# Filter units of a Hyena layer: whole fp32 transforms, small weights loaded on both partition halves, second buffers

## The chip, the cores and the metric

The kernel runs on one core of a Trainium2 chip. The metric is the device time of one execution in microseconds; lower is better. A core has TensorE (PE in the profile; its weight loads are PEld), VectorE (DVE), ScalarE (ACT) and GpSimd (POOL) for the work, and SyncE (SP), whose queue issues most of the transfers. Each engine works through its own instructions in order, and waits on semaphores where it needs another's result.

## What is computed

A trunk of two layers over 512 latent tokens and 256 context tokens, D = 1024, all in float32. Layer 0 is attention (a latent kind and a grouped-query kind side by side), layer 1 a Hyena mixer; each is followed by an MLP with squared ReLU and hidden width 4096. The change touches the part that prepares the Hyena filters:

```python
def hyena_filters(L, f_w1, f_b1, f_w2, f_b2, f_w3, f_b3, f_freq, f_w4):
    ...                                   # feats -> three sine layers -> h: (L, 64)
    h = (h @ f_w4.astype(F32)).reshape(L, 2, HYENA_ORDER, D_MODEL)
    ...
    h = h * window[:, None, None, :]
    h = h * lax.rsqrt(jnp.sum(h * h, axis=(0, 1), keepdims=True) + EPS)
    return h[:, 0], h[:, 1]

def bidir_long_conv(u, hf, hb, skip):
    L = u.shape[1]
    kfull = jnp.concatenate([hf, jnp.zeros_like(hf[:1]), hb[:0:-1]], axis=0)
    K = jnp.fft.rfft(kfull, n=2 * L, axis=0)
    U = jnp.fft.rfft(uf, n=2 * L, axis=1)
    y = jnp.fft.irfft(U * K[None], n=2 * L, axis=1)[:, :L]
    return (y + uf * skip.astype(F32)).astype(u.dtype)
```

There are two such convolutions, one after the other (orders n = 0 and 1), over all 1024 columns. `K` depends on the weights alone, not on the tokens.

## The kernel before

**Products.** Most products of the kernel are made of three products in a reduced format, fp32r: an operand is split into a part `hi` that fp32r holds and the remainder `lo`, and `mm3` (L107) adds hi x hi, hi x lo and lo x hi. A weight block is split by `split_w`: ScalarE casts `whi` (L125), VectorE subtracts to get `wlo` (L126). Activations are split by `split_to`: a cast (L169) and a subtraction (L172), which gives tiles such as `mHhi` and `mHlo` of the MLP's hidden values.

**Filter units.** The spectra `K` are made in eight units, one for each order n and each block c of 256 columns (`filter_unit`, from L984). A unit runs in steps:

1. It loads a row of `h_skip`, two blocks of `h_f_w4` (into `w4raw`, 64 partitions) and a block of the window. For the sum of the two directions (i = 0) it adds them to `w4s`, splits that into `w4hi` and `w4lo` on 64 partitions, and ScalarE copies both halves to partitions 64 to 127 (L1003, L1004), since the other operand `h3st` holds its high part in the lower and its remainder in the upper partitions. Eight products follow (L1012, L1013), and VectorE multiplies with the window into `eo0` (L1014).
2. The same for the difference (i = 1), into `eo1`. The tiles `w4s`, `w4hi`, `w4lo`, `w4raw`, `eo0` and `eo1` have one buffer each.
3. Squares and their sums (L1021, L1023); `eo0` and `eo1` are split into `eohi` and `eolo`.
4. The norm: one product (L1033), then a reciprocal root, and `skip` and `fy` are scaled.
5. The transforms to even and odd frequencies: twelve `mm3`, 36 products, of `eohi`/`eolo` with the tables `Tfhi`/`Tflo`, and one product of the `skip` row (L1060). VectorE makes the even part `kE` (L1065).
6. ScalarE copies the odd part `kO`, GpSimd merges both into `Kout` by four additions (L929), multiplies all with `fy` (L1072), and issues the store to DRAM (L1073). The Hyena layer reads it later.

**What sets the order.** The units lie beside the MLP of layer 0. The MLP gives out its products in blocks of 24, and after each block calls `tick` (L80), which takes one step from the list of background work. That is `zip_bg` (L1354): with each tick one step of the modulation for layer 1 (`mod_chunks`: a load of 512 KB, `modw`, on SyncE's queue, and one multiply-add on VectorE, L368 or L370) and one step of the filter units. So between the steps of a unit TensorE has one or two blocks of 24 MLP products. A scheduler then sets the order of instructions on each engine from the program's order and its own estimates. The transform tables are loaded by GpSimd's queue when the units begin.

Of the kernel before, what the change touches and what calls it, by code (L numbers as in the profile page):

```python
# [9 lines left out]
F32 = mybir.dt.float32  # L10
F32R = mybir.dt.float32r
AF = mybir.ActivationFunctionType
ALU = mybir.AluOpType
AX = mybir.AxisListType
P = 128

D, S, C, FF = 1024, 512, 256, 4096
# [48 lines left out]
def f(ap):  # L66
    return ap.bitcast(F32)


class Kernel:  # L70
# [839 lines left out]

    def load_tables(self, pool, inverse):

        nc, src = self.nc, self.a["k_dft"]
        res = []
        if inverse:
            for nm, sl in (("Tf", slice(0, 8)), ("Ti", slice(10, 22))):
                t = pool.tile([P, sl.stop - sl.start, P], F32, name=nm, bufs=1)
                nc.sync.dma_start(out=t, in_=src[:, 2, sl])
                res.append(t)
            return res  # L920
        t = Split(pool.tile([P, 10, P], F32R, name="Tfhi", bufs=1), pool.tile([P, 10, P], F32R, name="Tflo", bufs=1))
        nc.gpsimd.dma_start(out=t.hi, in_=src[:, 0, 0:10])
        nc.gpsimd.dma_start(out=t.lo, in_=src[:, 1, 0:10])
        return [t]

    def merge(self, U, E, O, e0, e1):

# [56 lines left out]
    def filter_unit(self, fp, T, n, c, kdst):  # L984

        nc, a = self.nc, self.a
        ch = slice(256 * c, 256 * c + 256)
        wf = fp.tile([65, 2, 256], F32, name="w4raw", bufs=1)
        nc.sync.dma_start(out=wf[64:65, 0], in_=a["h_skip"][0, n:n + 1, ch])
        for dr in range(2):  # L990
            nc.sync.dma_start(out=wf[0:64, dr], in_=a["h_f_w4"][0][:, (dr * 2 + n) * D + 256 * c:(dr * 2 + n) * D + 256 * c + 256])
        win = fp.tile([P, 4, 256], F32, name="win", bufs=1)
        nc.sync.dma_start(out=win, in_=a["k_win"][:, :, ch])
        skip = fp.tile([1, 256], F32, name="skip", bufs=2)
        nc.scalar.copy(skip, wf[64:65, 0])
        eo, spl = [], []
        for i, op in enumerate((ALU.add, ALU.subtract)):
            ws = fp.tile([64, 256], F32, name="w4s")
            nc.vector.tensor_tensor(out=ws, in0=wf[0:64, 0], in1=wf[0:64, 1], op=op)
            w2 = Split(fp.tile([P, 256], F32R, name="w4hi"), fp.tile([P, 256], F32R, name="w4lo"))  # L1000
            nc.scalar.copy(w2.hi[0:64], ws)
            nc.vector.tensor_tensor(out=w2.lo[0:64], in0=ws, in1=f(w2.hi[0:64]), op=ALU.subtract)
            nc.scalar.copy(w2.hi[64:128], f(w2.hi[0:64]))  # L1003
            nc.scalar.copy(w2.lo[64:128], f(w2.lo[0:64]))  # L1004
            e = fp.tile([P, 4, 256], F32, name=f"eo{i}", bufs=1)
            for t2 in range(2):
                ps = self.sm()
                for tt in range(2):
                    r = 2 * t2 + tt
                    lhs = self.h3[:, r * P:(r + 1) * P]  # L1010
                    o = ps[:, 256 * tt:256 * tt + 256]
                    nc.tensor.matmul(o, lhs, w2.hi, start=True, stop=False)  # L1012
                    nc.tensor.matmul(o, lhs, w2.lo, start=False, stop=True)  # L1013
                nc.vector.tensor_tensor(out=e[:, 2 * t2:2 * t2 + 2], in0=ps.rearrange("p (t n) -> p t n", t=2),  # L1014
                                        in1=win[:, 2 * t2:2 * t2 + 2], op=ALU.mult)
            eo.append(e)
            yield
# [6 lines left out]

        nc.vector.tensor_tensor(out=eo[0][0:1, 0], in0=eo[0][0:1, 0], in1=eo[1][0:1, 0], op=ALU.add)
        nc.vector.tensor_scalar(out=eo[0][0:1, 0], in0=eo[0][0:1, 0], scalar1=0.5, scalar2=None, op0=ALU.mult)
        for i in range(2):
            s = Split(fp.tile([P, 4, 256], F32R, name="eohi", bufs=2), fp.tile([P, 4, 256], F32R, name="eolo", bufs=2))
            self.split_to(s, eo[i])
            spl.append(s)  # L1030
        yield
        pn = self.sm()
        nc.tensor.matmul(pn, self.ones, sq[0], start=True, stop=True)  # L1033
# [16 lines left out]
        for b in (1, 0):  # L1050
            for i in (1, 0):
                o = pe[b][:, 256 * i:256 * i + 256]
                self.mm3(o, T[:, 4 * b + i], spl[i][:, 2 * b], True, bool(b or i))
        po = [self.sm() for _ in range(2)]
        for b in range(2):
            for i in range(2):
                q, cs = po[b][:, 256 * i:256 * i + 256], (i + b) % 2
                self.mm3(q, T[:, 2 + cs], spl[i][:, 1], True, False)
                self.mm3(q, T[:, 6 + 2 * b + cs], spl[i][:, 3], False, True)
        nc.tensor.matmul(o, self.ones[0:1], skip, start=False, stop=True)  # L1060
        c = fp.tile([P, 512], F32, name="kO1", bufs=1)
        nc.scalar.copy(c, pe[1])
# [340 lines left out]

def _r12(x):

    u = np.ascontiguousarray(x, np.float32).view(np.uint32).astype(np.uint64)
    u = (u + 0x7FF + ((u >> 12) & 1)) >> 12 << 12
    return u.astype(np.uint32).view(np.float32)  # L1410


def _tables():
    t = {}
    cst = np.zeros((P, 544), np.float32)
# [16 lines left out]
    for i, w in enumerate((HD, RP)):  # L1432
        nf = w // 4
        inv = (np.float32(10000.0) ** (-np.arange(nf, dtype=np.float32) / np.float32(nf))).astype(np.float32)
        for p in range(P):
            e = p % w
# [11 lines left out]
    tabs = [fn(ang(r)).T for r in range(4) for fn in (np.cos, np.sin)]  # L1448
    tabs += [-tabs[6], -tabs[7]]
    for eo in range(2):  # L1450
        for fn in (np.cos, np.sin):
            tabs += [fn(ang(eo)), fn(ang(eo + 2)), -fn(ang(eo + 2))]
    m = np.stack(tabs, 1).astype(np.float64)
    hi = _r12(m.astype(np.float32))
    t["k_dft"] = np.ascontiguousarray(np.stack([hi, _r12((m - hi).astype(np.float32)), m.astype(np.float32)], 1))

    tt = np.arange(S, dtype=np.float32)
    tn = tt / np.float32(S)
# [35 lines left out]
```

## Time and profile before

| | us |
|---|---|
| Median of 3 runs | 1568.7 (1565.3 to 1571.17) |
| Profiled execution | 1564.55 |
| Span of the trace | 1562.8 |
| TensorE busy in the span | 1449.0 (93%) |
| VectorE busy | 1109.5 (71%) |
| ScalarE busy | 699.7 (45%) |
| GpSimd busy | 403.1 (26%) |

The mean granted clock of TensorE is 0.976 of its full 2.4 GHz. The eight filter units lie between about 452 and 812 us of the span. In the profile an instruction is shown with its line, the tile that it writes, the tiles that it reads, and behind it in brackets the time that its engine stood idle before it and what ended that. `128*128 128x512` on a product is weights by moving columns; a product in plain fp32 is shown as two records.

### The profile page before, as it was taken

The page shows a single profiled execution, that of the slowest core. Times are in us where ns is not written, and L with a number is a line of the kernel's source. Part 1 is how long each engine was busy: PE and PEld are TensorE (multiplying, and loading weights), DVE is VectorE, ACT ScalarE, POOL GpSimd, SP SyncE. Part 2 cuts the span into 40 slices and gives each one's busy share as a digit, 9 for nine tenths or more (in the row PEclk, how much of TensorE's full clock was granted, in tenths as well). Part 3 has the DMA queues.
Part 4 walks back from the last instruction along what each step waited for, and adds up shares of the span by engine and source line. Part 5 has one row for each costly group of instructions (what it writes and reads, how often), then busy time and mean ns, then how long its engine had stood idle before and what let it go on. Part 6 is the DMA issues. An engine that isn't in the chain of part 4 may idle for free. (4 is left out here: it accounts for less than half of the span.)

```text
span 1562.8 us, 19761 instructions
## 1 busy us (share of the span) xinstructions
PE 1449.0 (93%) x7468; PEld 1192.0 (76%) x7468; DVE 1109.5 (71%) x1582; ACT 699.7 (45%) x1140; POOL 403.1 (26%) x340
## 2 busy tenths in 40 slices
PE   8688899999989999989999979999987999999998
PEld 2356588888877777878789967788776888888898
DVE  3898899887688988898765659798847434344454
ACT  3534587766653344344425444434325413232242
POOL 0440235232320322232220345445354000000001
PEclk9899999999999999999999989999998999999999
DMA  8557200221346655564334323231222223233241
GB/s 314 196 176 224 48 1 21 59 53 50 109 157 232 202 191 175 175 198 159 121 108 162 110 86 106 84 108 41 95 91 72 81 81 108 87 102 104 85 135 55
DMA packets 134461, 186.06 MB, mean 119 GB/s; under 512 B 16584, under 2 KB 117709, under 8 KB 131294
## 3 DMA queue, kind: packets, MB, share of 16 engines
q1 hardware_dynamic: 132192, 174.62, 34.6%
q0 software_dynamic: 1440, 9.70, 1.8%
q8 instruction: 59, 0.97, 0.3%
q10 hardware_dynamic: 734, 0.48, 0.1%
q14 instruction: 36, 0.29, 0.1%
HBM read 171.67 MB, written 10.49 MB: 117 GB/s over the span
## 5 line engine op out<-in xcount | busy, mean ns | idle before, releaser
L125 ACT CAST whi<-wraw 128x1024 fp32r<-128x1024 f32 (+3 forms) x211 | 198.9, 949 | 360.4 <-PE sm L110 341.1
L126 DVE TENSOR_TENSOR wlo<-wraw,whi 128x1024 fp32r<-128x1024 f32 (+2 forms) x195 | 241.4, 1242 | 105.8 <-ACT whi L125 95.8
L110 PE MATMUL sm<-h_lo,whi 128*128 128x512 f32 (+1 forms) x720 | 275.6, 384 | 3.9 <-POOL h_lo L424 3.1
L109 PE MATMUL sm<-h_hi,whi 128*128 128x512 f32 (+1 forms) x720 | 276.4, 387 | 2.2 <-ACT h_hi L420 2.2
L111 PE MATMUL sm<-h_hi,wlo 128*128 128x512 f32 (+1 forms) x720 | 274.1, 382 | 3.6 <-DVE wlo L126 3.6
L110 PE MATMUL sm<-mHlo,whi 128*128 128x512 f32 (+1 forms) x640 | 223.5, 349 | 6.0 <-DVE mHlo L172 6.0
L109 PE MATMUL sm<-mHhi,whi 128*128 128x512 f32 (+1 forms) x640 | 225.9, 353 | 0.5 <-ACT whi L125 0.3
L111 PE MATMUL sm<-mHhi,wlo 128*128 128x512 f32 (+1 forms) x640 | 223.2, 349 | 1.9 <-DVE wlo L126 1.9
L835 DVE SCALAR_TENSOR_TENSOR xT<-sm,mod,xT 128x512 f32<-128x512 f32 (+1 forms) x136 | 83.7, 621 | 150.7 <-PE sm L111 150.5
L110 PEld LDWEIGHTS sm<-h_lo,whi 128*128 128x128 f32 x720 | 136.0, 189 | 32.9 <-POOL h_lo L424 5.5
L111 PEld LDWEIGHTS sm<-h_hi,wlo 128*128 128x128 f32 x720 | 135.8, 189 | 32.1 <-DVE wlo L126 6.1
L109 PEld LDWEIGHTS sm<-h_hi,whi 128*128 128x128 f32 x720 | 134.8, 189 | 30.7 <-ACT h_hi L420 2.8
L110 PEld LDWEIGHTS sm<-mHlo,whi 128*128 128x128 f32 x640 | 121.7, 190 | 22.5 <-DVE mHlo L172 7.0
L111 PEld LDWEIGHTS sm<-mHhi,wlo 128*128 128x128 f32 x640 | 121.5, 190 | 18.7 <-DVE wlo L126 3.4
L109 PEld LDWEIGHTS sm<-mHhi,whi 128*128 128x128 f32 x640 | 121.4, 190 | 18.2 <-issue 1.7
L929 POOL TENSOR_TENSOR Kout<-kE,kO 128x512 f32<-128x512 f32 x32 | 46.3, 1471 | 264.6 <-DVE kE L1065 264.6
L370 DVE SCALAR_TENSOR_TENSOR modacc<-modw,silu,modacc 128x1024 f32<-128x1024 f32 x63 | 84.1, 1335 | 27.4 <-DMA modw<-in_w_mod 27.2
L1126 POOL TENSOR_TENSOR zx<-zx,zt 128x384 f32<-128x384 f32 x64 | 79.4, 1260 | 93.1 <-ACT zt L1124 91.8
L639 POOL TENSOR_SCALAR prob<-prob,smx 128x768 f32<-128x768 f32 x64 | 60.4, 943 | 146.9 <-DVE smx L638 91.8
L1245 POOL TENSOR_TENSOR facc<-facc,fsq 128x256 f32<-128x256 f32 x12 | 9.5, 790 | 333.1 <-ACT fsq L1243 333.1
L169 ACT CAST mHhi<-ms 128x512 fp32r<-128x512 f32 x64 | 39.6, 620 | 79.8 <-DVE ms L875 79.5
L637 ACT ACTIVATE prob<-big,smx,qry 128x768 f32<-128x768 f32 x64 | 63.7, 997 | 11.8 <-DVE smx L635 11.2
(458 smaller groups left out, 3002.4 us busy)
## 6 DMA issues: line engine op xcount, KB each, us to landing
wraw<-in_mlp_w SPq DMA_DIRECT2D x67, 1024.0 KB
modw<-in_w_mod SPq DMA_DIRECT2D x80, 512.0 KB
wraw<-in_h_w_in SPq DMA_DIRECT2D x12, 1024.0 KB
wm<-in_w_mod SPq DMA_DIRECT2D x8, 1024.0 KB
kd<-Kout POOLq DMA_DIRECT2D x8, 1024.0 KB, 5.4
Kin<-kd SPq DMA_DIRECT2D x8, 1024.0 KB
wraw<-in_a_w_in SPq DMA_DIRECT2D x5, 1024.0 KB
wraw<-in_a_w_out SPq DMA_DIRECT2D x9, 512.0 KB
```

The lines of the kernel that those rows point to most:

```text
L109: mm(ps, w.hi, x.hi, start=first, stop=False)
L110: mm(ps, w.hi, x.lo, start=False, stop=False)
L111: mm(ps, w.lo, x.hi, start=False, stop=last)
L125: nc.scalar.copy(hi, r3)
L126: (lo_eng or nc.vector).tensor_tensor(out=lo, in0=r3, in1=f(hi), op=ALU.subtract)
L169: nc.scalar.copy(dst.hi, src)
L370: nc.vector.scalar_tensor_tensor(out=acc, in0=w, scalar=s, in1=acc, op0=ALU.mult, op1=ALU.add)
L637: nc.scalar.activation(out=p, in_=sf, func=AF.Exp, bias=sm[:, 1:2], scale=sc, accum_out=sm[:, 2:3])
L639: nc.gpsimd.tensor_scalar(out=p, in0=p, scalar1=sm[:, 3:4], scalar2=1.0, op0=ALU.mult, op1=ALU.mult)
L835: nc.vector.scalar_tensor_tensor(out=xt, in0=ps, scalar=gcol[:, d:d + 1], in1=xt, op0=ALU.mult, op1=ALU.add)
L929: tt = lambda e, o, x, y, op: e.tensor_tensor(out=o, in0=x, in1=y, op=op)
L1126: nc.gpsimd.tensor_tensor(out=t[:, o0:o0 + n], in0=t[:, o0:o0 + n], in1=b[:, i0:i0 + n], op=ALU.add)
```

## The change

It does four things in the filter units:

- The transforms of step 5 are twelve products in plain fp32 rather than twelve `mm3`. The splits of `eo0` and `eo1` in step 3 are gone. The table is loaded once, in fp32 (`Tf`), by SyncE's queue, instead of `Tfhi` and `Tflo` by GpSimd's.
- `w4raw` has 128 partitions. Four loads bring each block of `h_f_w4` to both halves of the partitions; the sum or difference, the cast and the subtraction run over 128 partitions, and ScalarE's copies from half to half are gone. The row of `h_skip` comes by a load of its own rather than by way of `w4raw` and a copy.
- `w4raw`, `w4hi` and `w4lo` have two buffers.
- `eo0` and `eo1` have two buffers.

The rest of the diff follows from that: the table of the Hyena layer's own transforms is read from the same, smaller array.

```diff
     def load_tables(self, pool, inverse):
 
-        nc, src = self.nc, self.a["k_dft"]
         res = []
-        if inverse:
-            for nm, sl in (("Tf", slice(0, 8)), ("Ti", slice(10, 22))):
-                t = pool.tile([P, sl.stop - sl.start, P], F32, name=nm, bufs=1)
-                nc.sync.dma_start(out=t, in_=src[:, 2, sl])
-                res.append(t)
-            return res
-        t = Split(pool.tile([P, 10, P], F32R, name="Tfhi", bufs=1), pool.tile([P, 10, P], F32R, name="Tflo", bufs=1))
-        nc.gpsimd.dma_start(out=t.hi, in_=src[:, 0, 0:10])
-        nc.gpsimd.dma_start(out=t.lo, in_=src[:, 1, 0:10])
-        return [t]
+        for nm, sl in (("Tf", slice(0, 8)), ("Ti", slice(10, 22))) if inverse else (("Tf", slice(0, 10)),):
+            t = pool.tile([P, sl.stop - sl.start, P], F32, name=nm, bufs=1)
+            self.nc.sync.dma_start(out=t, in_=self.a["k_dft"][:, sl])
+            res.append(t)
+        return res
...
-        wf = fp.tile([65, 2, 256], F32, name="w4raw", bufs=1)
-        nc.sync.dma_start(out=wf[64:65, 0], in_=a["h_skip"][0, n:n + 1, ch])
+
+        wf = fp.tile([P, 2, 256], F32, name="w4raw", bufs=2)
         for dr in range(2):
-            nc.sync.dma_start(out=wf[0:64, dr], in_=a["h_f_w4"][0][:, (dr * 2 + n) * D + 256 * c:(dr * 2 + n) * D + 256 * c + 256])
+            for h in range(2):
+                nc.sync.dma_start(out=wf[64 * h:64 * h + 64, dr],
+                                  in_=a["h_f_w4"][0][:, (dr * 2 + n) * D + 256 * c:(dr * 2 + n) * D + 256 * c + 256])
         win = fp.tile([P, 4, 256], F32, name="win", bufs=1)
         nc.sync.dma_start(out=win, in_=a["k_win"][:, :, ch])
         skip = fp.tile([1, 256], F32, name="skip", bufs=2)
-        nc.scalar.copy(skip, wf[64:65, 0])
-        eo, spl = [], []
+        nc.sync.dma_start(out=skip, in_=a["h_skip"][0, n:n + 1, ch])
+        eo = []
         for i, op in enumerate((ALU.add, ALU.subtract)):
-            ws = fp.tile([64, 256], F32, name="w4s")
-            nc.vector.tensor_tensor(out=ws, in0=wf[0:64, 0], in1=wf[0:64, 1], op=op)
-            w2 = Split(fp.tile([P, 256], F32R, name="w4hi"), fp.tile([P, 256], F32R, name="w4lo"))
-            nc.scalar.copy(w2.hi[0:64], ws)
-            nc.vector.tensor_tensor(out=w2.lo[0:64], in0=ws, in1=f(w2.hi[0:64]), op=ALU.subtract)
-            nc.scalar.copy(w2.hi[64:128], f(w2.hi[0:64]))
-            nc.scalar.copy(w2.lo[64:128], f(w2.lo[0:64]))
-            e = fp.tile([P, 4, 256], F32, name=f"eo{i}", bufs=1)
+            ws = fp.tile([P, 256], F32, name="w4s")
+            nc.vector.tensor_tensor(out=ws, in0=wf[:, 0], in1=wf[:, 1], op=op)
+            w2 = Split(fp.tile([P, 256], F32R, name="w4hi", bufs=2), fp.tile([P, 256], F32R, name="w4lo", bufs=2))
+            self.split_to(w2, ws)
+            e = fp.tile([P, 4, 256], F32, name=f"eo{i}", bufs=2)
...
-        for i in range(2):
-            s = Split(fp.tile([P, 4, 256], F32R, name="eohi", bufs=2), fp.tile([P, 4, 256], F32R, name="eolo", bufs=2))
-            self.split_to(s, eo[i])
-            spl.append(s)
...
-                self.mm3(o, T[:, 4 * b + i], spl[i][:, 2 * b], True, bool(b or i))
+                nc.tensor.matmul(o, T[:, 4 * b + i], eo[i][:, 2 * b], start=True, stop=bool(b or i))
...
-                self.mm3(q, T[:, 2 + cs], spl[i][:, 1], True, False)
-                self.mm3(q, T[:, 6 + 2 * b + cs], spl[i][:, 3], False, True)
+                nc.tensor.matmul(q, T[:, 2 + cs], eo[i][:, 1], start=True, stop=False)
+                nc.tensor.matmul(q, T[:, 6 + 2 * b + cs], eo[i][:, 3], start=False, stop=True)
```

In the changed code the lines from L916 on are lower: `kE` is made at L1054, GpSimd's product with `fy` is L1061, the product of `skip` L1049, and the products with `w4lo` L1006.

On TensorE, the end of the first unit's transforms before; the numbers behind the tiles tell buffers apart:

```order
L109 MATMUL sm_5101<-eohi_4995,Tfhi_4816 128x256
L110 MATMUL sm_5101<-eolo_4996,Tfhi_4816 128x256
L111 MATMUL sm_5101<-eohi_4995,Tflo_4817 128x256
L109 MATMUL sm_5101<-eohi_4999,Tfhi_4816 128x256
L110 MATMUL sm_5101<-eolo_5000,Tfhi_4816 128x256
L111 MATMUL sm_5101<-eohi_4999,Tflo_4817 128x256
L1060 MATMUL sm_5086<-skip_4870,ones_79 128x256
```

The same place after:

```order
L1047 MATMUL sm_5080<-eo0_4877,Tf_4816 128x256
L1048 MATMUL sm_5080<-eo0_4877,Tf_4816 128x256
L1047 MATMUL sm_5080<-eo1_4925,Tf_4816 128x256
L1048 MATMUL sm_5080<-eo1_4925,Tf_4816 128x256
L1049 MATMUL sm_5073<-skip_4869,ones_79 128x256
```

Three products have become one, which reads `eo` itself; the blocks of the MLP around them stand as before.

On VectorE, around the first unit's `kE` before. `xT` is the stream that the MLP adds to, `modacc` the modulation's sum, and `w4lo_5244` the remainder for the second unit's second group of products:

```order
L368 TENSOR_SCALAR modacc_6083<-modw_6084,silu_105 128x1024
L1065 TENSOR_TENSOR kE0_5129<-sm_5086,kO1_5127 128x512
L1065 TENSOR_TENSOR kE1_5131<-sm_5086,kO1_5127 128x512
L370 SCALAR_TENSOR_TENSOR modacc_6083<-modw_6170,silu_105,modacc_6083 128x1024
L370 SCALAR_TENSOR_TENSOR modacc_6083<-modw_6239,silu_105,modacc_6083 128x1024
L835 SCALAR_TENSOR_TENSOR xT_76<-sm_5133,mod0_2_95,xT_76 128x512
L1014 TENSOR_TENSOR eo0_5189<-sm_5190,win_5177 128x512
L1014 TENSOR_TENSOR eo0_5189<-sm_5196,win_5177 128x512
L126 TENSOR_TENSOR wlo_5209<-wraw_5202,whi_5208 128x1024
L1002 TENSOR_TENSOR w4lo_5244<-w4s_5241,w4hi_5243 64x256
```

The same place after; `w4lo_5454` is for the third unit's first group:

```order
L368 TENSOR_SCALAR modacc_5965<-modw_5966,silu_105 128x1024
L370 SCALAR_TENSOR_TENSOR modacc_5965<-modw_6028,silu_105,modacc_5965 128x1024
L1054 TENSOR_TENSOR kE0_5092<-sm_5073,kO1_5090 128x512
L1054 TENSOR_TENSOR kE1_5094<-sm_5073,kO1_5090 128x512
L370 SCALAR_TENSOR_TENSOR modacc_5965<-modw_6096,silu_105,modacc_5965 128x1024
L370 SCALAR_TENSOR_TENSOR modacc_5965<-modw_6154,silu_105,modacc_5965 128x1024
L835 SCALAR_TENSOR_TENSOR xT_76<-sm_5096,mod0_2_95,xT_76 128x512
L1007 TENSOR_TENSOR eo0_5151<-sm_5152,win_5141 128x512
L1007 TENSOR_TENSOR eo0_5151<-sm_5158,win_5141 128x512
L126 TENSOR_TENSOR wlo_5171<-wraw_5164,whi_5170 128x1024
L172 TENSOR_TENSOR w4lo_5454<-w4s_5451,w4hi_5453 128x256
```

A step of the modulation has moved ahead of `kE`, and the `w4lo` behind it is that of a later group.

On VectorE after, the place where the remainder for the second unit's second group now stands, ahead of the first unit's norm and 24 rows ahead of `kE`:

```order
L1019 TENSOR_SCALAR eo0_4877<-eo0_4877 1x256
L1016 TENSOR_TENSOR kE0_4977<-kE0_4977,kO0_4979 128x512
L172 TENSOR_TENSOR w4lo_5206<-w4s_5203,w4hi_5205 128x256
L370 SCALAR_TENSOR_TENSOR modacc_5358<-modw_5617,silu_105,modacc_5358 128x1024
L835 SCALAR_TENSOR_TENSOR xT_76<-sm_4948,mod0_2_95,xT_76 128x512
```

The remainder has moved from behind the transforms to ahead of the norm, and the `eolo` pair that stood there is gone.

## Rows read from the trace of the kernel before

**Rows 1.** Windows; columns: stretch, length, busy time of each engine, PEclk, DMA share, GB/s.

```profile
452.00:812.00 360.00, 341.17 (x1627) 280.00 (x1627) 302.52 (x386) 152.24 (x242) 90.13 (x49) 0.98 0.55 178
580.00:600.00 20.00, 20.00 (x86) 16.14 (x86) 19.62 (x32) 11.51 (x19) 0.00 (x0) 0.92 0.67 217
600.00:620.00 20.00, 16.85 (x87) 13.97 (x87) 16.07 (x17) 7.71 (x15) 11.21 (x6) 0.93 0.35 112
620.00:640.00 20.00, 20.00 (x86) 16.44 (x86) 17.76 (x29) 7.67 (x12) 0.00 (x0) 0.90 0.57 176
...
700.00:720.00 20.00, 20.00 (x89) 16.48 (x88) 19.34 (x30) 11.62 (x19) 0.00 (x0) 0.93 0.62 204
```

**Rows 2.** PE's waits, 452 to 812: line waited for, us in all, times, longest.

```profile
PE sm L1013 <- ACT w4lo L1004: 9.4, 6, 4.3
...
PE sm L110 <- DVE mHlo L172: 6.0, 3, 3.1
...
PE sm L111 <- DVE wlo L126: 3.1, 4, 1.1
...
PE sm L109 <- ACT mHhi L169: 0.2, 1, 0.2
```

**Rows 3.** Timeline of PE, single waits: start, length, instruction, [idle before, its releaser].

```profile
540.14 0.38 PE L1013 MATMUL sm<-w4lo,h3st 128*128 128x256 f32 x1 [2.42 <-ACT w4lo L1004]
...
554.56 0.50 PE L111 MATMUL sm<-h_hi,wlo 128*128 128x512 f32 x1 [1.11 <-DVE wlo L126]
...
578.87 0.39 PE L1013 MATMUL sm<-w4lo,h3st 128*128 128x256 f32 x1 [1.84 <-ACT w4lo L1004]
...
618.53 0.80 PE L110 MATMUL sm<-mHlo,whi 128*128 128x512 f32 x1 [3.15 <-DVE mHlo L172]
...
672.76 0.50 PE L111 MATMUL sm<-h_hi,wlo 128*128 128x512 f32 x1 [0.72 <-DVE wlo L126]
...
699.47 0.58 PE L1013 MATMUL sm<-w4lo,h3st 128*128 128x256 f32 x1 [4.26 <-ACT w4lo L1004]
...
810.02 0.50 PE L111 MATMUL sm<-h_hi,wlo 128*128 128x512 f32 x1 [0.19 <-DVE wlo L126]
```

**Rows 4.** Timeline of POOL, DVE and ACT, 692 to 700.

```profile
692.65 5.39 POOL L1072 TENSOR_TENSOR Kout<-Kout,fy 128x2048 f32<-128x2048 f32 x1
...
693.77 4.82 DVE L172 TENSOR_TENSOR mHlo<-ms,mHhi 128x512 fp32r<-128x512 f32 x1
...
698.51 0.41 DVE L1002 TENSOR_TENSOR w4lo<-w4s,w4hi 64x256 fp32r<-64x256 f32 x1
...
699.01 0.40 ACT L1004 CAST w4lo<-w4lo 64x256 fp32r<-64x256 f32 x1 [5.27 <-DVE w4lo L1002]
```

**Rows 5.** Line L1072: times, ns min/median/max, first and last start.

```profile
L1072 POOL TENSOR_TENSOR Kout<-Kout,fy x8: 4584/4614/5477, 533.6 to 804.3; 128x2048 f32<-128x2048 f32 x8
```

**Rows 6.** Timeline of PE, first unit: first transform product, and the product of `skip`.

```profile
520.40 0.28 PE L109 MATMUL sm<-eohi,Tfhi 128*128 128x256 f32 x1
...
524.80 0.69 PE L1060 MATMUL sm<-skip,ones 1*128 1x256 f32 x2
```

**Rows 7.** Timeline of PE in the Hyena layer, whole fp32 products, eight records a row.

```profile
975.79 1.89 PE L1187 MATMUL sm<-Ti,E 128*128 128x256 f32 x8
...
977.52 1.89 PE L1187 MATMUL sm<-Ti,O 128*128 128x256 f32 x8
```

**Rows 8.** Groups by line, 452 to 812: busy us, mean ns, idle before.

```profile
L172 DVE TENSOR_TENSOR eolo<-eo,eohi 128x1024 fp32r<-128x1024 f32 x16 | 18.9, 1214 | 0.8 <-ACT eohi L169 0.8
...
L169 ACT CAST eohi<-eo 128x1024 fp32r<-128x1024 f32 x16 | 16.0, 1048 | 9.3 <-DVE eo L1026 9.3
```

**Rows 9.** DVE's wait for the modulation's loads (waits view), and its timeline in unit 5.

```profile
DVE modacc L370 <- DMA modw<-in_w_mod: 23.0, 12, 4.1
...
684.43 0.75 DVE L368 TENSOR_SCALAR modacc<-modw,silu 128x1024 f32<-128x1024 f32 x1 [1.81 <-DMA modw<-in_w_mod]
...
685.70 1.28 DVE L1065 TENSOR_TENSOR kE<-sm,kO 128x512 f32<-128x512 f32 x2
```

More of the change, by code (lines that the diff above doesn't have):

```diff
@@ L1402, in build @@
                         pass
[L1406 to L1410, printed above, removed]
 def _tables():
@@ L1452, in _tables @@
             tabs += [fn(ang(eo)), fn(ang(eo + 2)), -fn(ang(eo + 2))]
-    m = np.stack(tabs, 1).astype(np.float64)
-    hi = _r12(m.astype(np.float32))
-    t["k_dft"] = np.ascontiguousarray(np.stack([hi, _r12((m - hi).astype(np.float32)), m.astype(np.float32)], 1))
+    t["k_dft"] = np.ascontiguousarray(np.stack(tabs, 1).astype(np.float32))
     tt = np.arange(S, dtype=np.float32)
```

## The prediction, made before the change was run

> **What bounds the kernel now.** I read the windows of the stretch in which the filter units run first, then TensorE's waits in it, then those waits one by one in the timeline, and last what VectorE and GpSimd did meanwhile. The stretch lasts 360.00 us. TensorE is busy for 341.17 of it, VectorE for 302.52, ScalarE for 152.24 and GpSimd for 90.13 [rows 1]. So TensorE sets the end, and a microsecond is gained only where TensorE waits, runs longer, or runs at a lower clock. About 18.8 us are waits, and three lines account for nearly all: `w4lo` 9.4, `mHlo` 6.0, `wlo` 3.1 [rows 2]. All three are remainders that VectorE makes (`w4lo` then passes once more through ScalarE, which copies it to the upper partitions). The reader should see in the timeline that the waits are few and long, and that the long ones sit at the same place of a unit, some 13 us behind its transforms [rows 3].
>
> What holds VectorE there? GpSimd's product `Kout` x `fy` at L1072 runs 5.39 us from 692.65. VectorE's subtraction `mHlo` starts at 693.77, takes 4.82 us and ends at 698.59, just behind GpSimd's end at 698.04. The `w4lo` behind it needs 0.41, its copy 0.40, and only then does TensorE go on [rows 4]. L1072 comes eight times, of 4.58 to 5.48 us [rows 5]. A VectorE operation with two SBUF inputs that meets it does not finish before it does.
>
> TensorE's clock is the second loss. Behind three of the long waits the granted clock of the next 20 us is 0.92, 0.93, 0.93, and 0.90 in the stretch that follows the second; it was 0.98 over the whole [rows 1]. Part of each such stretch ran at 1.2 GHz rather than 2.4. With TensorE 20 us busy these cost 20 x 0.08 = 1.6 (580 to 600, behind the `w4lo` wait at 578.87), 20 x 0.07 = 1.4 (700 to 720, behind that at 699.47), and 1.4 + 2.0 = 3.4 (600 to 640, around the `mHlo` wait at 618.53).
>
> **The change part by part.** All terms stand against the profiled execution, 1564.55 us, which is 4.15 below the median of 1568.7; I add that at the end.
>
> Transforms. The trace of before has 36 products in 520.40 to 524.80, 4.40 us a unit [rows 6]. After, there are 12 whole fp32 products, each of two records. The Hyena layer has the same form: eight records of 128x256 take 977.52 - 975.79 = 1.73 us, 0.216 each [rows 7]. 24 x 0.216 = 5.18, so +0.78 a unit and **+6.3** for eight.
>
> The Trainium skill, "FP8 and Floating Point Precision", section "TensorE Precision Notes", says that a true FP32 product takes four passes. At the pace of before's products, 4.40 / 36 = 0.122, a product would take 0.49; rows 7 show 2 x 0.216 = 0.43, so the trace is near the rule and a little below it. What the difference would make is the fifth case below.
>
> `w4lo`. Four things go: the two ScalarE copies to the upper partitions, the single buffers of `w4hi`, `w4lo` and `w4raw`. With two buffers the second group's `w4lo` of the next unit stands some 24 rows ahead of `kE` on VectorE, where it stood 6 to 8 rows behind it, inside GpSimd's L1072. What now stands behind `kE` belongs to the unit after next. All six waits go: **-9.4** [rows 2], of which 2.42 + 1.84 + 4.26 = 8.5 are three [rows 3]. The added waits are for four small loads instead of two; with the second buffer they are issued a unit earlier, and what queues behind the addition on VectorE would be the next `wlo`.
>
> Splits of `eo`. VectorE loses 16 x 1.21 us and ScalarE 16 x 1.05 [rows 8]. Most of it is time in which nobody waited. Twice TensorE waited for a `wlo` that stood behind such a pair: 1.11 at 554.56 and 0.72 at 672.76 [rows 3]. **-1.8**.
>
> What comes late next. GpSimd's product stays, and VectorE still stops in it. TensorE's next need is the `wlo` of the following weight block, which VectorE makes behind the stopped operation. The nearest row is the eighth unit, which has no `w4lo` behind it: TensorE waited 0.19 for `wlo` at 810.02 [rows 3]. Eight such are 1.5, the lower bound; the upper one is the whole 9.4 again. I take **+3.0**, near the lower end, as the two units whose product came latest (waits of 3.15 and 4.26) should pay more than 0.19.
>
> Clock. If the two long `w4lo` waits are gone, the 1.2 GHz stretches behind them should go as well: **-3.0** (1.6 + 1.4). Bounds: 0, where another wait takes their place, and -6.4, where the 3.4 around the `mHlo` wait go too.
>
> At nothing: ScalarE's removed casts and copies (its 152.24 of 360 us are its cover, and it is waited for almost only through `w4lo`); the row of `skip`; `Tf` by SyncE's queue, 4 bytes an element once rather than twice. `Tf` goes ahead of the first `modw`, and each unit issues two more DMAs on that queue; no TensorE wait in rows 2 names a DMA, and if that cover is gone it is the fourth case. The second `eo` buffers are the price of keeping `eo` until the transforms, and cost no time.
>
> Sum: 6.3 - 9.4 - 1.8 + 3.0 - 3.0 = -4.9, so 1559.65 for such an execution and 1559.65 + 4.15 = **1563.8**. A measurement of this kernel can tell about 0.5%, 7.8 us, from no change: 1560.9 to 1576.5 is "same".
>
> **The rivals.** Second, everything that is late on VectorE goes: no stand-in wait, the `mHlo` wait of 3.15 too, and all clock stretches: 6.3 - 9.4 - 1.8 - 3.15 - 6.4 = -14.45, **1554.3**. For it: VectorE has 19 us less to do, and starts `kE` and what follows with less in its queue. Against it: L1072 is untouched, and `mHlo` and `wlo` are still due in its 5 us.
>
> Third, the change does not do what it says: GpSimd's hold moves whole to the next remainder. Then 9.4 comes back as `wlo` and `mHlo` waits with their clock stretches: 6.3 - 1.8 = +4.5, **1573.2**. For it: rows 4, where the stopped operation is not `w4lo` at all but the one ahead of it. Against it: at 810.02 only 0.19 was left without a `w4lo` [rows 3].
>
> The Trainium skill, "SBUF — State Buffer", section "Who interferes with whom", states that a VectorE instruction with two SBUF inputs contends with a GpSimd instruction that reads SBUF, over an exclusive lock in which the first to issue wins. The trace agrees (4.82 us for `mHlo`), and by that rule removing work elsewhere leaves the lock where it is, which is this third case.
>
> Fourth, slower: a wait for `modw` ahead of `kE`. In units 1, 2, 3, 5 and 6 one or two more steps of the modulation (L370) stand ahead of `kE` on VectorE than before. Such a step waits for 512 KB on SyncE's queue: 23.0 us in 12 waits, a mean of 1.92. In unit 5 it has happened already: VectorE waited 1.81 at L368, and `kE` started only at 685.70 [rows 9], the longest `w4lo` wait followed. With the third case's sum, 4.5 + 5 x 1.92 = +14.1, **1582.8**. It decides from about two such units on (4.5 + 2 x 1.92 = 8.3, over the 7.8). Against it: VectorE has two microseconds and more free in each unit from the splits that are gone.
>
> Fifth, whole fp32 products at four passes of before's pace: 4 x 0.122 x 12 = 5.86, +1.46 a unit and +11.7 rather than 6.3. The forecast would be 5.4 later, **1569.2**. Rows 7 speak against it.
>
> **How the numbers follow.** Forecast 0.42, second 0.28, third 0.13, fourth 0.11, fifth 0.06. The likeliest gives 1563.8. With its bounds (1.5 for the late remainder and -6.4 for the clock) the forecast itself reaches down to -9.8 + 4.15, 1558.9, and I give 0.08 of its 0.42 to "faster"; upwards, at 9.4 and 0, it reaches 1573.2. Faster: 0.28 + 0.08 = 0.36. Slower: 0.11, and 0.01 for a forecast that misses upwards: 0.12. Same: the rest, 0.52. The range goes from 1552.0, a little below the second case, to 1576.0, above the third; it leaves out the fourth.
>
> **What the trace of after would show.** The transforms at 24 records of about 0.216, 5.2 us a unit; if 5.9, the fifth case. No waits at the second group for `w4lo`, and `w4lo` on VectorE some 10 us or more ahead of `kE`. L1061, GpSimd's product, still of 4.6 us or longer, with one VectorE operation of 4 to 5 us in it eight times. TensorE's waits for `wlo` and `mHlo` from 452 on near 3 + 6 in sum (second case: under 3; third: 15 or more). A granted clock of 0.98 or more for the 20 us behind the places of 578.87 and 699.47. For the fourth case: VectorE waiting for `modw` in front of `kE`, and `kE` two microseconds or more behind the row of `skip`. The prediction is wrong in its main step if the `w4lo` waits are still there, or if time changes outside this stretch.

## The result, and the profile after

The changed kernel takes 1580.4 us in the median of four runs beside 1567.1 of before, a ratio of 1.0086 (1.0059 to 1.0113). Measured again beside the experiments it took 1582.1 to 1569.1, 1.0096 (1.0067 to 1.0124). It is slower by some 13 us. The forecast was 1563.8, in a range up to 1576; the nearest of the rivals was the fourth, 1582.8.

Its profiled execution took 1577.04 us, span 1575.3, against 1564.55 and 1562.8 before. I laid the residual additions of the MLPs in the two traces side by side. The changed kernel is 2.5 us later when the units begin, and this grows by 7.3 in the stretch of the units and by 2.8 behind it. The first 2.5 are not the change's: the code there is the same, and over all profiles of this study this stretch scatters from 1.0 less to 6.1 more than in the profile of before, which was among the early ones. Over the units the changed kernel's second profile shows 10.9 more. What follows is about the 7 to 11 us of the units.

The windows of the changed kernel, columns as in [rows 1]:

```profile
452.00:830.00 378.00, 357.00 (x1582) 289.42 (x1582) 291.99 (x378) 123.41 (x193) 91.37 (x49) 0.98 0.53 173
540.00:560.00 20.00, 17.44 (x69) 13.54 (x68) 18.69 (x25) 5.11 (x9) 2.15 (x2) 0.91 0.73 253
580.00:600.00 20.00, 20.00 (x90) 16.23 (x89) 16.58 (x27) 7.41 (x13) 0.03 (x1) 1.00 0.64 210
600.00:620.00 20.00, 15.68 (x71) 12.13 (x69) 14.49 (x20) 7.42 (x13) 8.32 (x5) 1.00 0.40 132
620.00:640.00 20.00, 17.21 (x71) 14.24 (x72) 13.91 (x22) 5.07 (x7) 2.78 (x2) 0.83 0.46 159
700.00:720.00 20.00, 16.08 (x72) 12.43 (x71) 18.53 (x22) 8.13 (x14) 4.30 (x2) 1.00 0.66 213
740.00:760.00 20.00, 16.16 (x65) 12.27 (x64) 13.94 (x18) 7.07 (x11) 5.87 (x3) 0.91 0.38 132
```

The stretches at 580 and 700, behind the two `w4lo` waits of before, are now at full clock. The one behind the `mHlo` wait is worse: 0.83 in 620 to 640, where [rows 1] had 0.90. And the stretches at 540 and 740, at 1.00 before, are at 0.91, behind a wait of 2.56 us for `wlo` (548.51) and one of 3.61 for `mHhi` (750.30). In windows of 20 us from 452 to 832, each counted as 20 us times what its clock lacks of 1.00, the lower clock comes to 8.8 us before and 8.6 in the changed kernel: it has moved and not shrunk.

TensorE's waits in the units, to compare with [rows 2] (line waited for, us in all, times, longest):

```profile
PE sm L109 <- ACT mHhi L169: 7.3, 3, 3.6
...
PE sm L111 <- DVE wlo L126: 6.9, 5, 3.4
...
PE sm L110 <- DVE mHlo L172: 5.0, 3, 3.5
...
PE sm L1049 <- DVE skip L1033: 1.5, 2, 0.9
```

`w4lo` is gone from the list, as forecast. But the sum is 20.7 us, where it was 18.7: `mHhi` rose from 0.2 to 7.3, `wlo` from 3.1 to 6.9, and a wait for the `skip` row is new. From the first unit's product of `skip` to the eighth's the changed kernel takes 8.2 us more (280.9 for 272.7). About 6 of these are the dearer transforms of seven units, shown next; the rest are waits.

The transforms, first unit (TensorE's timeline; `x8` are eight records), beside [rows 6]:

```profile
521.05 1.89 PE L1042 MATMUL sm<-eo,Tf 128*128 128x256 f32 x8
522.78 0.59 PE L1047 MATMUL sm<-eo,Tf 128*128 128x256 f32 x2
...
526.33 0.69 PE L1049 MATMUL sm<-skip,ones 1*128 1x256 f32 x2
```

Eight records take 1.73 us as forecast; the whole takes 5.28 rather than 4.40.

GpSimd's product stands as it stood in [rows 5]:

```profile
L1061 POOL TENSOR_TENSOR Kout<-Kout,fy x8: 4508/4622/5491, 535.9 to 814.0; 128x2048 f32<-128x2048 f32 x8
```

The third unit shows how its hold, and one thing more, reach TensorE. The timeline of all engines, transforms' end at 603.95:

```profile
603.95 0.48 PE L1049 MATMUL sm<-skip,ones 1*128 1x256 f32 x1 [0.89 <-DVE skip L1033]
...
607.84 1.28 DVE L370 SCALAR_TENSOR_TENSOR modacc<-modw,silu,modacc 128x1024 f32<-128x1024 f32 x1 [2.01 <-DMA modw<-in_w_mod]
...
610.81 1.25 DVE L1054 TENSOR_TENSOR kE<-sm,kO 128x512 f32<-128x512 f32 x2
...
611.61 6.00 POOL L923 TENSOR_TENSOR Kout<-kE,kO 128x512 f32<-128x512 f32 x4 [31.58 <-DVE kE L1054]
...
617.63 0.63 ACT L1014 ACTIVATE kE<-eo 128x512 f32<-128x512 f32 x1 [2.61 <-POOL Kout L923]
...
617.68 4.51 POOL L1061 TENSOR_TENSOR Kout<-Kout,fy 128x2048 f32<-128x2048 f32 x1
...
618.17 0.60 ACT L169 CAST mHhi<-ms 128x512 fp32r<-128x512 f32 x1
...
618.80 3.93 DVE L172 TENSOR_TENSOR mHlo<-ms,mHhi 128x512 fp32r<-128x512 f32 x1 [2.32 <-ACT mHhi L169]
618.83 0.50 PE L109 MATMUL sm<-mHhi,whi 128*128 128x512 f32 x1 [2.75 <-ACT mHhi L169]
...
622.79 0.79 PE L110 MATMUL sm<-mHlo,whi 128*128 128x512 f32 x1 [3.46 <-DVE mHlo L172]
```

VectorE waits 2.01 us for a load of the modulation and starts `kE` 6.86 us behind the transforms' end. GpSimd's merge starts that much later. ScalarE's squares of the next unit are written into the tiles named `kE` and `kO`, which the merge still reads, so ScalarE stands 2.61 us, with `mHhi` queued behind. `mHlo` can then start only when GpSimd's product has begun, and is held for 3.93. TensorE pays 2.75 + 3.46. In units 3, 5 and 6 `kE` starts 6.86, 4.89 and 5.77 us behind the transforms' end (2.24, 3.42 and 0.73 before); in the other five it is 1.63 us or less. Not all of this lag is a wait for a load. Behind the transforms' end VectorE waits 2.01, 0.30 and 0.80 us for `modw` in these units; the rest is work that stands ahead of `kE`, in units 3 and 6 also the transpose of the modulation's sum (L373, 1.24 us), which was not ahead of it before.

### The profile page after: what moved, and what is told of

The parts are those of the page before. It is cut to its first block, busy times and chain, and to the rows that moved or that the text cites. A ratio compares the mean times of both kernels' runs of the same rounds, so it can differ in the third digit from the quotient of the medians.

```text
span 1575.3 us, 19531 instructions
## 1 busy us (share of the span) xinstructions
PE 1460.3 (93%) x7372; PEld 1198.0 (76%) x7372; DVE 1093.7 (69%) x1566; ACT 665.7 (42%) x1084; POOL 402.6 (26%) x338
## 5 line engine op out<-in xcount | busy, mean ns | idle before, releaser
L126 DVE TENSOR_TENSOR wlo<-wraw,whi 128x1024 fp32r<-128x1024 f32 (+2 forms) x195 | 244.7, 1258 | 111.0 <-ACT whi L125 98.9
L370 DVE SCALAR_TENSOR_TENSOR modacc<-modw,silu,modacc 128x1024 f32<-128x1024 f32 x63 | 84.0, 1333 | 32.3 <-DMA modw<-in_w_mod 31.9
L172 DVE TENSOR_TENSOR mHlo<-ms,mHhi 128x512 fp32r<-128x512 f32 x64 | 50.5, 792 | 30.9 <-ACT mHhi L169 30.5
```

Of the source, the lines that this page charges most:

```text
L126: (lo_eng or nc.vector).tensor_tensor(out=lo, in0=r3, in1=f(hi), op=ALU.subtract)
L172: (lo_eng or nc.vector).tensor_tensor(out=dst.lo, in0=src, in1=f(dst.hi), op=ALU.subtract)
L370: nc.vector.scalar_tensor_tensor(out=acc, in0=w, scalar=s, in1=acc, op0=ALU.mult, op1=ALU.add)
```

## The experiments

Times are medians beside runs of the kernel before on the same chip, 1567.7 to 1569.1 in the four sets. "Lag" is the time from the product of `skip` to `kE`; "units" the time from the first unit's product of `skip` to the eighth's in the profile: 272.7 us before, 280.9 and 282.4 in two profiles of the changed kernel. The intervals of the ratios reach 3 to 5 us to either side, so a difference of a few microseconds between two of the variants is not shown.

**The two parts alone.** The small weights, in the kernel before (`w4raw` keeps one buffer and a norm's scratch tile moves into `kE1`'s, since the split tiles leave no room):

```diff
+        wf = fp.tile([P, 2, 256], F32, name="w4raw", bufs=1)    # four loads, skip by its own
...
+            w2 = Split(fp.tile([P, 256], F32R, name="w4hi", bufs=2), fp.tile([P, 256], F32R, name="w4lo", bufs=2))
+            self.split_to(w2, ws)
-        t_ = fp.tile([P, 256], F32, name="ft")
+        t_ = fp.tile([P, 512], F32, name="kE1", bufs=1)[:, 0:256]
```

> The kernel before with only the part on the small weights: four loads to both halves, one cast and one subtraction over 128 partitions, two buffers for w4hi and w4lo (w4raw keeps one, for lack of room). Transforms as before, 36 products. Theory A (the small weights gain what was forecast, and the loss of the whole change comes from the transforms and from kE that comes late behind modw): the 9.4 us of w4lo waits go, 3 to 5 come back as wlo and mHlo waits, time 1560 to 1563 beside 1567 of before. Theory B (GpSimd's hold passes whole to the next remainder): the sum of TensorE's waits from 452 to 812 stays near 18.8 us, time 1566 to 1568.

Measured: 1567.4, ratio 0.9994 (0.9974 to 1.0013); units 272.2. TensorE's waits from 452 to 815:

```profile
PE sm L111 <- DVE wlo L126: 9.9, 10, 2.3
...
PE sm L110 <- DVE mHlo L172: 4.3, 3, 2.5
...
PE sm L1058 <- DVE skip L1042: 2.7, 2, 1.9
...
PE sm L109 <- ACT mHhi L169: 1.9, 2, 1.0
```

They sum to 18.8 (18.7 before), without one `w4lo`. Time and sum are theory B's: the 9.4 us came back in full on other tiles. That GpSimd's hold is what carried them is not shown by that; a run further down tests it.

The transforms alone (whole products, no splits, two `eo` buffers, one table), the small weights as before:

```diff
-                self.mm3(o, T[:, 4 * b + i], spl[i][:, 2 * b], True, bool(b or i))
+                nc.tensor.matmul(o, T[:, 4 * b + i], eo[i][:, 2 * b], start=True, stop=bool(b or i))
```

> The kernel before with only the transforms as whole fp32 products: no splits of eo, two buffers for eo, one table by SyncE's queue; the small weights as before. Theory A: the transforms cost 0.87 us a unit, 7.0 in all, less 1.8 for the wlo waits behind the split pairs: 1572 to 1573, w4lo waits still near 9. Theory C (the transforms carry the whole loss, since without the splits VectorE runs into the modulation's loads ahead of kE): kE 4 us and more behind the skip product in two units or more, 1578 to 1581.

Measured: 1577.0, 1.0071 (1.0043 to 1.0099); units 279.8, of which the products are 7 x 0.87 = 6.1. The lag is 4.80 in unit 1 and 6.19 in unit 3. The timeline of VectorE in unit 1, and TensorE's wait that follows:

```profile
529.33 0.75 DVE L368 TENSOR_SCALAR modacc<-modw,silu 128x1024 f32<-128x1024 f32 x1 [1.35 <-DMA modw<-in_w_mod]
530.63 1.28 DVE L370 SCALAR_TENSOR_TENSOR modacc<-modw,silu,modacc 128x1024 f32<-128x1024 f32 x1 [0.55 <-DMA modw<-in_w_mod]
531.84 1.28 DVE L1056 TENSOR_TENSOR kE<-sm,kO 128x512 f32<-128x512 f32 x2
...
539.77 4.50 POOL L1063 TENSOR_TENSOR Kout<-Kout,fy 128x2048 f32<-128x2048 f32 x1
...
546.23 0.58 PE L1008 MATMUL sm<-w4lo,h3st 128*128 128x256 f32 x1 [6.31 <-ACT w4lo L999]
```

Two steps of the modulation wait in front of `kE`, and `w4lo` then costs 6.31 where the same place of before cost 2.42 [rows 3]. The time lies between the two theories, 1 us from C, whose sign of two late `kE` is there. But 7.0 of the 8.9 us are the products, and the rest lies within the interval. The wait for `wlo` behind the split pairs went as theory A had it, from 3.1 us to 0.9:

```profile
PE sm L111 <- DVE wlo L126: 0.9, 1, 0.9
```

The changed kernel once more:

> The changed kernel once more, beside the following runs and with more executions. The two parts alone gave -0.7 us (small weights) and +8.9 us (transforms). If the parts add up, 1575 to 1577. If they work against each other (the transforms make kE late, and the second buffers let the modulation's loads run into it), 1579 to 1581.

Measured: 1582.1, as above. The parts alone give -0.7 and +8.9, so the whole lies some 5 us above their sum. With intervals of 3 to 5 us on each of the three that isn't clear of the noise. The small weights alone also differ from their part of the change, by `w4raw`'s one buffer and the place of the scratch tile.

**Late loads of the modulation.** Four buffers for `modw`; the room is what the splits of `eo` left:

```diff
-                            self.mod_bufs = 2
+                            self.mod_bufs = 4
```

> The changed kernel with four buffers for modw instead of two, so that the modulation's loads are issued earlier. Theory A: no wait for modw in front of kE, kE within 2 us of the skip product in all units, the mHhi waits of 2.75 and 3.61 gone, 1573 to 1575 beside 1580. Theory B: kE earlier, but TensorE's waits for wlo and mHlo take the place, 1578 to 1581.

Measured: 1564.6, 0.9987 (0.9971 to 1.0004), 16 to 17 us below the changed kernel and 8 below what theory A asked; units 272.3. `kE` is not within 2 us in all units: the lag is 3.61 in unit 2 and 5.00 in unit 3. VectorE's waits for `modw` fall from 29.3 us to 12.7 (L370 and L368 below), and from unit 4 on the lag is 0.8 or less and no wait of TensorE over 0.25 us is left. In the first three units `wlo` and `mHlo` are still late:

```profile
PE sm L111 <- DVE wlo L126: 7.9, 5, 3.7
DVE modacc L370 <- DMA modw<-in_w_mod: 7.1, 5, 2.8
DVE modacc L368 <- DMA modw<-in_w_mod: 5.6, 3, 3.0
PE sm L110 <- DVE mHlo L172: 4.2, 2, 4.0
PE sm L109 <- ACT mHhi L169: 1.1, 1, 1.1
```

More steps of the modulation stand ahead of `kE` here (44, 55, 64, 71 in units 1 to 4 against 42, 50, 56, 58), and yet `kE` is earlier. So it is not their number that costs; fewer of them stand waiting for a load.

One load that all steps read:

```diff
+                    if l and i == 0 and k == 0 and not hasattr(self, "once"):
+                        self.once = self.modp.tile([P, 1024], F32, name="modonce", bufs=1)
...
+                    if l:
+                        w = self.once
```

> The changed kernel with one load of the modulation's weights for layer 1, which all 48 steps then read: the other 47 loads of 512 KB are left out, the steps on VectorE stay, and the output is another. Theory A (late modw is what makes kE, the squares and mHhi late): no waits for mHhi and for the skip product, kE within 2 us of the skip product in all eight units, 1560 to 1565. If late modw is not the cause, 1577 and more.

Measured: 1560.7, 0.9955 (0.9936 to 0.9975); units 269.4. No wait for `mHhi` is left, one of 0.8 us for `skip`, and the lag is under 2.5 us everywhere; `wlo` alone still costs 9.3 us. Theory A holds, nearly, for `kE`, `skip` and `mHhi`: late loads made them late. It does not hold for `wlo`. This run also takes 47 transfers off the queue (the DMA engines' share falls from 0.53 to 0.35 from 452 to 815), so it does not tell lateness from traffic. Four buffers keep all the loads and gave 16 to 17 of these 20 us or so.

The steps in another order:

```diff
-                            self.bg = [self.zip_bg(mods, gens)]
+                            self.bg = [self.zip_bg(gens, mods)]
```

> The changed kernel with the filter units' step ahead of the modulation's in each tick. On VectorE 41, 50, 56, 58, 65, 71 steps of the modulation then stand ahead of the kE of units 1 to 6, instead of 42, 50, 56, 58, 66, 72 (41, 49, 54, 58, 65, 70 before). If one step more ahead of kE is what makes it late, kE of units 1, 5 and 6 comes within 3.5 us of the skip product and that of unit 3 stays 6 to 7 us behind it, 3 to 6 us below the changed kernel. If the loads are late however the steps stand, no difference.

Measured: 1579.2, 1.0071 (1.0048 to 1.0094), not to be told from the changed kernel. The lag is 2.69, 4.53 and 2.10 in units 1, 5 and 6, and 6.55 in unit 3. Of the three named, unit 6 alone came forward. The count of steps ahead of `kE`, which the fourth rival went by, is a poor guide.

**The squares' tiles.**

```diff
-        sq = [fp.tile([P, 512], F32, name=nm, bufs=1) for nm in ("kE0", "kE1", "kO0", "kO1")]
+        sq = [fp.tile([P, 512], F32, name=nm, bufs=1) for nm in ("sq0", "sq1", "sq2", "sq3")]
```

> The changed kernel with tiles of their own for the squares, which in it share the buffers of kE and kO, so that ScalarE's squares of the next unit wait for GpSimd's merge of this one. Theory A: the mHhi waits of 2.75 and 3.61 us come through that wait and go, together with their stretches at 1.2 GHz, while the modw waits stay: 4 to 7 us below the changed kernel. If mHhi is late for another reason, no difference.

Measured: 1578.2, 1.0068 (1.0043 to 1.0093); the difference to the changed kernel, 4 us, lies within the two intervals. ScalarE no longer waits for GpSimd's merge, and TensorE's waits for `mHhi` fall from 7.3 and 5.5 in two profiles to 2.8. But `wlo` rises to 11.5. The path was rightly seen, and it was worth little by itself.

**GpSimd's long instruction.** The product in eight pieces, in the changed kernel:

```diff
-        nc.gpsimd.tensor_tensor(out=K, in0=K, in1=y.unsqueeze(1).broadcast_to([P, 8, 256]), op=ALU.mult)
+        for r in range(8):
+            nc.gpsimd.tensor_tensor(out=K[:, r], in0=K[:, r], in1=y, op=ALU.mult)
```

> The changed kernel with GpSimd's product Kout x fy cut into eight of 128x256. If GpSimd's one long instruction is what holds VectorE, no VectorE operation of 512 or 1024 columns takes more than about 2 us in the units, TensorE's waits for wlo and mHlo fall from 11.9 us to 3 or less, and the time to 1570 to 1573; the mHhi waits (7.3 us) stay. If the hold goes by GpSimd's work and not by the instruction, VectorE still loses 4 to 5 us in each unit, and the time stays at 1579 to 1582.

> A second look at the changed kernel with GpSimd's product in eight pieces, whose first profile was of its slowest execution. No VectorE operation of 4 us and more in the units, TensorE's waits for wlo and mHlo under 7 us; modw and mHhi waits as they fall.

Measured: 1567.8, 1.0005 (0.9987 to 1.0022), 13 to 14 us below the changed kernel and below the 1570 to 1573 expected, and 1565.4 in one more execution. The longest VectorE operation in the units is 2.2 us; the changed kernel has eight of 3.8 to 5.2. Waits for `wlo` and `mHlo` sum to 6.6 and 6.4 us in the two profiles, where 3 or less was expected, for `mHhi` to 8.7 and 5.5. The pieces are dearer for GpSimd, 64 of 0.92 us (median) for eight of 4.6, and still gain: what holds VectorE is the length of one instruction.

The same in the kernel before:

> The kernel before, with GpSimd's product Kout x fy in eight pieces of 128x256 and nothing else. If that one long instruction is what makes w4lo and mHlo late, the 9.4 us of w4lo waits and the longest mHlo wait go: 1553 to 1560 beside 1568. If the hold comes back in pieces, 1565 to 1569.

Measured: **1554.2, 0.9918 (0.9888 to 0.9948)**, the lowest median of all, though three others below lie within its interval; units 261.1, 11.6 less than before. Its waits, and the same place as 618.53 in [rows 3]:

```profile
PE sm L111 <- DVE wlo L126: 3.8, 5, 1.4
PE sm L1013 <- ACT w4lo L1004: 3.4, 2, 2.9
PE sm L109 <- ACT mHhi L169: 2.5, 2, 2.2
PE sm L110 <- DVE mHlo L172: 2.1, 2, 1.8
...
616.57 4.88 POOL L1073 TENSOR_TENSOR Kout<-Kout,fy 128x256 f32<-128x256 f32 x3
617.13 0.72 DVE L172 TENSOR_TENSOR mHlo<-ms,mHhi 128x512 fp32r<-128x512 f32 x1 [2.33 <-ACT mHhi L169]
617.77 0.94 DVE L1002 TENSOR_TENSOR w4lo<-w4s,w4hi 64x256 fp32r<-64x256 f32 x1
```

`mHlo` takes 0.72 and `w4lo` 0.94 while GpSimd multiplies beside them. The `w4lo` waits fall from 9.4 to 3.4 with single buffers and the copies still in place. Waits are a little over half of the gain in the units: they sum to 11.8 us where they were 18.7. Nearly all the rest is the clock, whose loss, counted as above, falls from 8.8 us to 3.6.

**Where the small weights' gain went.** Their part with the pieces:

> The part on the small weights alone, with GpSimd's product in eight pieces. If the small weights gained nothing because the hold passed to wlo and mHlo, the pieces set that gain free: 1553 to 1558, and below the kernel before with pieces by what w4lo still waits for there. If the pieces do all of it, the same time as that kernel.

Measured: 1567.4, 0.9993 (0.9969 to 1.0017), 13 us above the kernel before with pieces. A miss: freed of GpSimd's long instruction, the part costs as much as the pieces gain. Its waits:

```profile
PE sm L111 <- DVE wlo L126: 9.4, 7, 2.6
PE sm L110 <- DVE mHlo L172: 3.1, 2, 2.5
PE sm L109 <- ACT mHhi L169: 3.0, 2, 2.8
PE sm L1058 <- DVE skip L1042: 2.6, 2, 1.4
```

`wlo` and the `skip` row carry it, 12.0 us against 3.8. In all the waits are 18 us as in the part with the whole product, and the clock's loss is 9.0 us against 3.6, though no VectorE operation in the units takes more than 2.1 us. So theory B's reason does not hold by itself: the waits stand here without the long instruction. In this run VectorE also stands 6.0 us, in three waits, for the loads of `w4raw` (1.1 in the kernel before with pieces); the changed kernel, with two buffers for it, shows no such wait. Two runs take the part apart: the loads to both halves with one buffer each, and the second buffers with 64 partitions and the copies. Both keep the scratch tile in `kE1`'s buffer and one buffer for `w4raw`.

```diff
+            w2 = Split(fp.tile([P, 256], F32R, name="w4hi"), fp.tile([P, 256], F32R, name="w4lo"))          # e13
+            w2 = Split(fp.tile([P, 256], F32R, name="w4hi", bufs=2), fp.tile([P, 256], F32R, name="w4lo", bufs=2))  # e14
```

> GpSimd's product in eight pieces, and of the small weights' part only the loads to both halves: one buffer each for w4raw, w4hi and w4lo, so that on VectorE w4lo stands behind kE as before. Theory D (the second buffers bring w4lo and w4s forward on VectorE, ahead of the wlo and the skip row that TensorE needs sooner): no loss without them, 1552 to 1557. If the loads to both halves are what costs, about 1567 as with the whole part.

> GpSimd's product in eight pieces, and of the small weights' part only the second buffers of w4hi and w4lo: loads, cast, subtraction and ScalarE's copies on 64 partitions as before. Theory D: the loss is here, 1564 to 1568, with TensorE's waits for wlo and for the skip product as in the whole part. If the loads are what costs, 1552 to 1557.

Measured: 1561.6, 0.9956 (0.9939 to 0.9973), and 1558.4, 0.9940 (0.9922 to 0.9958). Beside 1554.2 these are +7.5 and +4.2; the first lies 1 to 2 us outside that run's interval, with intervals that overlap, and the second inside it. Theory D, one place for all of the loss, is not borne out: it came in two parts, or between them, or in part from the scratch tile, which no run moved alone. By which step `wlo` becomes late was not settled.

**The transforms with pieces.** Alone, then with one buffer for `eo` and four for `modw`:

> The transforms' part alone with GpSimd's product in eight pieces. Beside the kernel before with pieces (1554) the transforms cost 7.0 us of TensorE: 1561 if that is all; 1563 and more if kE comes late behind modw as in the transforms' part alone, where kE of units 1 and 3 stood 4.8 and 6.2 us behind the skip product.

> The same with one buffer for eo0 and eo1 and four for modw. If late modw is what is left, 1555 to 1559, no kE more than 5 us behind the skip product; if the four buffers gain nothing once the product is in pieces, as the run before it.

Measured: 1567.2, 0.9988 (0.9971 to 1.0006), and 1556.7, 0.9924 (0.9904 to 0.9944). The first is the second of its two cases, with a lag of 5.84 in unit 3; the second lies in the range, but the lag in unit 3 is still 6.15. So beside 1554.2 the transforms cost 11 to 13, of which 7 are products; four buffers for `modw` and one for `eo` give back 10.6. No run tried four buffers in the kernel before, where the splits take the room.

Everything together, on the changed kernel: `eo` with one buffer, own tiles for the squares, four buffers for `modw`, pieces.

> The changed kernel with one buffer for eo0 and eo1 again, tiles of their own for the squares, four buffers for modw, and GpSimd's product in eight pieces. Theory A: TensorE waits under 4 us in the units, which leaves the transforms' +7.0 and takes 18.8 us of waits: 1555 to 1560. If four buffers for modw had already taken all that can be had, 1563 to 1566.

Measured: 1559.4, 0.9945 (0.9927 to 0.9964); units 266.4, waits of 7.8 us in three lines (`skip` 4.4, `wlo` 2.6, `mHlo` 0.8), where under 4 was expected. It beats both kernels. The kernel before with nothing but the pieces has the lower median, but the two intervals overlap.

## Why the prediction was wrong

The term that failed is the one for what comes late next, priced at +3.0; in the changed kernel it measured +11.4. The clock's -3.0, which hung on it, came to nothing. The other terms were near or small.

**Transforms, +6.3: right, a little short.** They cost +0.87 a unit, 7.0 in all. The records have the forecast 0.216; the 0.09 more is the step from the last transform to the product of `skip`, which the 4.40 of before contains and 24 x 0.216 leaves out. The fifth case (5.86 us a unit) fell.

**`w4lo`, -9.4: the step was right, its worth was not.** All six waits went. With the small weights alone, 18.8 us of waits stood on other tiles.

**What comes late next, +3.0: this is the term that failed.** It measured +9.4 with the small weights alone, where the sum of the waits did not change, and 20.7 - (18.7 - 9.4) = +11.4 in the changed kernel. I took it from the one unit without a `w4lo` behind GpSimd's product, 0.19 us, and read that as what the following `wlo` needs. But there the operation that GpSimd held was that very `wlo`, for 5.13 us:

```profile
804.83 5.13 DVE L126 TENSOR_TENSOR wlo<-wraw,whi 128x1024 fp32r<-128x1024 f32 x1 [5.21 <-ACT whi L125]
```

It ended at 809.96, and TensorE, which went on at 810.02, had come to it only 0.19 us before. So the 0.19 is what was left at one place where TensorE came late, and not the price of a hold. In every unit of the changed kernel GpSimd's product holds one VectorE operation with two SBUF inputs: `wlo` at 5.17, 5.16 and 4.69 us, `w4lo` at 4.84, `mHlo` at 4.04 and 3.93, and two more `wlo` of 4.20 and 3.79. The Trainium skill, "SBUF — State Buffer", section "Who interferes with whom", which I had set beside the third rival, says that such an instruction contends with a GpSimd instruction that reads SBUF. The traces agree: the eight end 0.3 to 1.1 us behind GpSimd's product, and in the changed kernel with pieces no VectorE operation in the units takes more than 2.2 us.

The hold is not the whole of what failed here. Late loads of the modulation are the other part: four buffers for them, with GpSimd's product as it was, took the waits from 20.7 us to 13.8 and 16 to 17 us off the time. And with the small weights alone the waits came back even without a long instruction.

**Splits, -1.8: right where the transforms stand alone.** There `wlo` went from 3.1 to 0.9. In the whole change it rose to 6.9, for the reasons above.

**Clock, -3.0: not found.** The two stretches behind the `w4lo` waits came back to 1.00, but two others fell to 0.91 and the one at 620 to 640 to 0.83, each behind a wait that took the place of those that went. Over the units the loss is 8.6 us where it was 8.8. This is the bound of 0 that the term had.

**The fourth rival** came out closest, 1582.8 beside 1580.4 and 1582.1, with 0.11 of the chance. Its place was right in three of the five units named (3, 5 and 6). Its price was not: VectorE's waits for `modw` as a whole hardly grew (29.3 and 33.3 us in two profiles, 28.2 before), so that the sum with 5 x 1.92 comes within 2.4 us of the measured times is luck. What grew is what a late `kE` drags along, the merge, the squares that share its tiles, and `mHhi`; by itself the sharing of the tiles was not worth more than the noise. I had not followed that chain, since in the trace of before ScalarE waited for the merge once, for 0.5 us. Nor was the rival's measure, the number of steps ahead of `kE`, the cause: four buffers raise that number and take the loss away.

**Range and chances.** 1552 to 1576 left the fourth case outside. With the late remainder at its upper bound, which [rows 4] pointed to, and the clock at 0, the sum is 1573.2, and what the waits for `modw` add belongs on top of it. With the terms as measured, 7.0 for the transforms, -9.4, +11.4 with the splits in it and 0 for the clock, the sum is +9.0 and 1577.7. Of the 3 to 4 us that are left, 2.8 and 1.7 lie behind the units in the two profiles.

**Open:** why the small weights' part costs 13 us once the long instruction is gone, and so how much of the 11.4 is GpSimd's hold; and some 2 us behind the units, which most kernels with whole fp32 transforms show (0.6 to 3.6 in twelve profiles, -1.5 to 1.7 in those without).

## What to carry to other kernels

When a wait is removed behind a resource that holds an engine for a fixed time, price the change by the hold and not by the waiter: the next operation can inherit it. Look first for the hold itself; here one instruction of 4.6 us cut into eight gave 13 us in the kernel before and in the changed one, 10 to 13 with the transforms alone, and nothing with the small weights alone. So its worth is no fixed sum. A load that arrives just in time for a step in an in-order queue is a stall waiting for a place: four buffers for it, instead of two, gave 16 to 17 us in the changed kernel. And count the clock with the waits: some two fifths of what the pieces gave in the units of the kernel before was clock.

## What had not been expected of the hardware

Cutting GpSimd's product into pieces makes it dearer (64 pieces with a median of 0.92 us in the changed kernel, where an eighth of the whole is 0.58) and the kernel faster. VectorE and GpSimd then share the time: `wlo` takes 1.7 to 1.9 us beside the pieces, where it takes 1.2 alone and up to 5.2 beside the whole. In the kernel before with pieces it is GpSimd that now stands: its pieces have a median of 0.74 us, but the longest takes 9.00. And kernels whose code is the same up to 434 us differ there by up to 7 us from profile to profile, and by 3 to 4 us between two executions of one kernel; a difference of one profile from another is worth less than that unless it is taken from stretch to stretch.
